# Gate and up of a gated MLP by Strassen's seven products for half of their K pairs, in an fp32 two-block kernel on one core

## The chip, the cores and the metric

One core of one Trainium2 chip runs the whole program as one launch. The metric is device time in microseconds (us). TensorE (PE) multiplies, VectorE (DVE), ScalarE (ACT) and GpSimd (POOL) do the elementwise work, SyncE (SP) issues the loads; POOL can issue loads as well.

## The reference

Two transformer blocks in fp32 on 256 tokens of width 2048 (16 meta tokens in front in the first block). What the change computes anew is the second block's gated MLP:

```python
def swiglu(h, w_gate, w_up, w_down):
    return (jax.nn.silu(h @ w_gate) * (h @ w_up)) @ w_down

def second_block(x, ...):
    h = h + hybrid_mixer(rms_norm(h, norm_mix[l]), ...)   # ends in: m @ w_out
    h = h + swiglu(rms_norm(h, norm_ffn[l]), w_gate[l], w_up[l], w_down[l])
    return rms_norm(h, norm_final)
```

w_gate and w_up are 2048 x 5632, w_down is 5632 x 2048, w_out is 2048 x 2048.

## The kernel before

Every fp32 product with weights is made of three products of parts: a number x is split into xh (12 significant bits) and xl (the rest), and x w is taken as xh wh + xh wl + xl wh. `load` fetches a piece of weights of 128 x 1024 (wr, 512 KB, issued by SP at L293), ACT copies it to the high part wh (L296), DVE subtracts to get the low part wl (L297). Raw pieces have 5 buffers, wh and wl 3 each, in one pool for the whole kernel.

Two shapes of product follow. `gemm_a` keeps weights stationary and streams 256 to 272 token columns (L304 to L306). `gemm_b` keeps 128 tokens stationary and streams 512 weight columns (L311 to L313) into one bank of PSUM for each of two token tiles. PSUM has four banks of tag g and four of tag a; a tag's banks go round in the order of first use in the program.

The second block ends like this. `branch` makes the three branches' outputs in four column blocks j; a branch's product is scaled on DVE (L979) and added to m on POOL (L980). For the last branch each j spawns `turn`, which transposes m on PE (L908) and splits it on ACT (L274) and DVE (L275) into mt. Then w2out (the mixing projection) runs over mt for four j, its result is added to the residual tiles htok (L1062), and another `turn` makes xn3, split and scaled, the input of the MLP.

`feed_forward_2` walks the 44 tiles of hidden width in two parts of 24 and 20. In a part, each block b (512 hidden columns, 11 in all) multiplies xn3 with gate (banks of tag g) and up (banks of tag a), 96 matmuls of 512 columns each; ACT applies silu straight from PSUM (L1087), DVE multiplies up's sums in (scalar_tensor_tensor, "stt", L1088) to get sl, and `turn` makes from it four split tiles at, with two banks of tag a and eight transposes. Then the part's down product over at follows for four column blocks, and DVE adds it to htok (L1104). The tail is a norm and the stores.

The program's order sets priorities; a scheduler orders each engine's instructions by it ahead of time, among those that are ready by its own costs. Work such as `turn` is spawned with a delay and placed between the steps of the large products. An engine runs its list in that order, so an instruction that waits holds all behind it.

The first block's end matters too. The last heads' attention runs while the first products of w1out (`gemm_a`, output blocks f) already stand between; `product(f)` in `mixing_1` is called ahead for f = 1 and 2, and the residual tiles ht are loaded by SP at L801.

## Time and profile before

| what | value |
|---|---|
| time, median of 3 runs | 2778.96 us (2778.73 to 2779.33) |
| span of the profiled execution | 2777.6 us |
| PE busy | 2760.7 us (99%) |
| DVE busy | 1573.4 us (57%) |
| ACT busy | 1292.5 us (47%) |
| POOL busy | 275.3 us (10%) |
| moved by DMA | 498.30 MB, mean 179 GB/s |

Busy time is the time in which an engine has work under way. PE's matmuls are pipelined: a matmul's own duration is longer than the distance to the next one's start, so the pace is read from starts in a timeline. The granted clock is 1.00 where the throttle gives TensorE its full 2.4 GHz. Durations of single instructions come from one profiled execution.

### The profile page before, as it was taken

What the parts mean: (1) busy time and instruction counts of PE and PEld (TensorE: products, weight loads), DVE (VectorE), ACT (ScalarE), POOL (GpSimd) and SP (SyncE); (2) the same over time, 40 slices, a digit from 0 to 9 for tenths busy, and PEclk for the clock granted to TensorE, in tenths of its full rate; (3) what the DMA queues carried; (4) which work ended last, traced back from release to release, by engine and by line L of the source; (5) the groups of instructions that cost most, each with busy time, mean ns of one, the idle gap of its engine ahead of it and who ended that gap; (6) DMA issues with size and microseconds to landing.
All of it is one profiled execution on the core that took longest, in us unless ns stands there. A gap on an engine that the chain in (4) does not pass through costs nothing.

```text
span 2777.6 us, 40930 instructions
## 1 busy us (share of the span) xinstructions
PE 2760.7 (99%) x16346; PEld 2425.5 (87%) x16346; DVE 1573.4 (57%) x2006; ACT 1292.5 (47%) x1768; POOL 275.3 (10%) x304
## 2 busy tenths in 40 slices
...
GB/s 234 161 125 120 109 195 182 183 182 184 188 189 183 184 185 185 182 181 178 182 189 185 192 188 170 168 180 184 182 182 189 182 189 183 188 189 184 190 195 151
DMA packets 142035, 498.30 MB, mean 179 GB/s; under 512 B 15890, under 2 KB 17427, under 8 KB 141843
## 3 DMA queue, kind: packets, MB, share of 16 engines
...
q8 instruction: 128, 2.10, 0.3%
q10 hardware_dynamic: 434, 0.78, 0.1%
...
## 4 chain that ended last, share of the span: by engine, by line
PE 99%; POOL 0%; DVE 0%; ACT 0%; DMA 0%; issue 0%; ACTq 0%; SPq 0%; POOLq 0%; DVEq 0%
PE ps L311 19%; PE ps L313 19%; PE ps L312 19%; PE ps L304 13%; PE ps L305 12%; PE ps L306 12%; PE ps L908 1%; PE ps L601 1%; PE ps L685 0%; PE ps L686 0%; PE ps L603 0%; PE ps L644 0%; POOL ht L811 0%; PE ps L574 0%; PE ps L1171 0%; DVE wl L297 0%
## 5 line engine op out<-in xcount | busy, mean ns | idle before, releaser
L297 DVE TENSOR_TENSOR wl<-wr,wh 128x1024 fp32r<-128x1024 f32 (+2 forms) x937 | 1148.7, 1227 | 1000.0 <-ACT wh L296 998.5
L296 ACT ACTIVATE wh<-wr 128x1024 fp32r<-128x1024 f32 (+2 forms) x937 | 979.8, 1046 | 1259.6 <-PE ps L313 788.2
L311 PE MATMUL ps<-wh,xn 128*128 128x512 f32 x1216 | 483.1, 397 | 0.0
L313 PE MATMUL ps<-wh,xn 128*128 128x512 f32 x1216 | 479.6, 394 | 0.0
L312 PE MATMUL ps<-wl,xn 128*128 128x512 f32 x1216 | 478.6, 394 | 0.0
L305 PE MATMUL ps<-xf,wh 128*128 128x258 f32 (+1 forms) x1408 | 398.2, 283 | 0.0
L304 PE MATMUL ps<-xf,wh 128*128 128x258 f32 (+1 forms) x1408 | 397.9, 283 | 0.0
L306 PE MATMUL ps<-xf,wl 128*128 128x258 f32 (+1 forms) x1408 | 396.1, 281 | 0.0
L311 PE MATMUL ps<-wh,at 128*128 128x512 f32 x704 | 278.9, 396 | 0.0
L313 PE MATMUL ps<-wh,at 128*128 128x512 f32 x704 | 277.6, 394 | 0.0
L312 PE MATMUL ps<-wl,at 128*128 128x512 f32 x704 | 277.4, 394 | 0.0
L313 PEld LDWEIGHTS ps<-wh,xn 128*128 128x128 f32 x1216 | 228.1, 188 | 54.4
L312 PEld LDWEIGHTS ps<-wl,xn 128*128 128x128 f32 x1216 | 228.5, 188 | 52.2
L311 PEld LDWEIGHTS ps<-wh,xn 128*128 128x128 f32 x1216 | 228.3, 188 | 51.6
L306 PEld LDWEIGHTS ps<-xf,wl 128*128 128x128 f32 x1408 | 267.8, 190 | 0.0
L305 PEld LDWEIGHTS ps<-xf,wh 128*128 128x128 f32 x1408 | 265.8, 189 | 0.1
L304 PEld LDWEIGHTS ps<-xf,wh 128*128 128x128 f32 x1408 | 265.0, 188 | 0.1
L304 PE MATMUL ps<-xn,wh 128*128 128x256 f32 x640 | 181.9, 284 | 0.0
L305 PE MATMUL ps<-xn,wh 128*128 128x256 f32 x640 | 179.7, 281 | 0.0
L306 PE MATMUL ps<-xn,wl 128*128 128x256 f32 x640 | 179.5, 280 | 0.0
L313 PEld LDWEIGHTS ps<-wh,at 128*128 128x128 f32 x704 | 132.2, 188 | 31.8
L311 PEld LDWEIGHTS ps<-wh,at 128*128 128x128 f32 x704 | 132.3, 188 | 30.7
...
## 6 DMA issues: line engine op xcount, KB each, us to landing
wr<-in_w1ff SPq DMA_DIRECT2D x176, 512.0 KB, 3.3
wr<-in_w2g SPq DMA_DIRECT2D x96, 512.0 KB, 3.4
wr<-in_w1down SPq DMA_DIRECT2D x88, 512.0 KB, 3.3
wr<-in_w2gate SPq DMA_DIRECT2D x88, 512.0 KB, 3.3
wr<-in_w2up SPq DMA_DIRECT2D x88, 512.0 KB, 3.3
wr<-in_w2down SPq DMA_DIRECT2D x88, 512.0 KB, 3.3
wr<-in_w2a SPq DMA_DIRECT2D x80, 512.0 KB, 3.3
wr<-in_w1in SPq DMA_DIRECT2D x48, 512.0 KB, 3.3
```

What stands on the lines that cost most here:

```text
L296: self.last_copy = nc.scalar.activation(h[:, d], raw[:, d], AF.Copy)
L297: nc.vector.tensor_tensor(l[:, d], raw[:, d], h[:, d].bitcast(F32), op=OP.subtract)
L304: mm(ps, wh, xh, start=first, stop=False)
L305: mm(ps, wh, xl, start=False, stop=False)
L306: mm(ps, wl, xh, start=False, stop=last)
L311: mm(ps, xh, wh, start=first, stop=False)
L312: mm(ps, xh, wl, start=False, stop=False)
L313: mm(ps, xl, wh, start=False, stop=last)
L601: PE.matmul(ps[:, :257], v01[:, b * 128:b * 128 + 128], ta[:, b * 257:b * 257 + 257], start=b == 0, stop=False)
L908: self.nc.tensor.transpose(ps[:, i * 256 + t * 128:i * 256 + t * 128 + 128], tiles[t][:, f * 128:f * 128 + 128], self.cs("ident"))
```

## The change

For four of the eight K pairs (two tiles of 128 rows each; `FAST` = pairs 0, 2, 4, 6) of gate and up, the 2 x 2 block product of (two token tiles) x (two K tiles) x (two halves of 256 columns) is made by Strassen's scheme with seven products instead of eight, in the form with shared sums. Each of the seven is again three products of parts, each with 128 x 128 stationary and 256 columns streaming (L1171). The other four pairs go on as before.

- The token side's sums are made once, in `turn_fast`: the transposed, scaled tile is copied to a raw tile, three subtractions follow, and four splits.
- The weight side's sums are made for each piece, in `load_fast`: SP loads y (128 x 512: two blocks' copies of b12) and x (128 x 768: b11, b21, b22), POOL issues a load of 128 x 512 that adds into y on arrival, and DVE makes two more sums of 256 columns (L1140, L1141). ACT and DVE then split 1024 columns of x and 768 of y (ACT L1143, DVE L1144).
- The result is put together at the end of a block in `gemm_fast`: own banks (tag g) take products that belong to one quarter alone, sums banks (tag a) the shared ones; two ACT copies (L1177) and seven DVE operations (L1180 to L1186) combine them. Silu and the stt read and write SBUF tiles then.
- Gate, then silu, then up, then the stt, each with two banks of either tag. The down product goes in four parts of 12, 12, 12 and 8 tiles.
- Pools: weights of attention_1 have their own; a pool `ph` holds the eight residual tiles; mixing_1 to mixer_2 use `wp2` and `p2`; w2out and the MLP use `wp3` (raw 6, wh and wl 5 each) and `p3`.

Comments and debug calls are left out of the diff, as are lines that only follow from them.

```diff
...
 FFN_PARTS = (24, 20)
-
-# columns of the packed vectors
+FFN_PARTS_2 = (12, 12, 12, 8)
...
+def pack_fast(w):
+
+
+
+    k, n = w.shape
+    b = w.reshape(k // 256, 2, 128, n // 512, 2, 256).transpose(3, 0, 1, 4, 2, 5)
+    f = b[:, list(FAST)]
+    b11, b12, b21, b22 = (f[:, :, i, j] for i in range(2) for j in range(2))
+    rest = [p for p in range(k // 256) if p not in FAST]
+    r = w.reshape(k // 256, 2, 128, n // 512, 512).transpose(3, 0, 2, 1, 4)[:, rest]
+    cat = lambda *x: np.concatenate(x, axis=-1)
+    return cat(b11, b21, b22), cat(b12, b12), cat(b11, b22), r.reshape(r.shape[:3] + (1024,))
+
...
-    f["w2gate"] = pack_b(i["w_gate_2"][0])
-    f["w2up"] = pack_b(i["w_up_2"][0])
+    for k, v in (("w2gate", "w_gate_2"), ("w2up", "w_up_2")):
+        for x, p in zip("xyap", pack_fast(i[v][0])):
+            f[k + x] = p
...
     def mid(self, name, w=512, dtype=F32):
-        tag, bufs = ("m1", 10) if w <= LP else ("m15", 8) if w <= 384 else ("m2", 17)
-        return self.p2.tile([128, w], dtype, name=name, tag=tag, bufs=bufs)
+        i = 0 if w <= LP else 1 if w <= 384 else 2 if w <= 2 * LP else 3
+        return self.p2.tile([128, w], dtype, name=name, tag="m%d" % i, bufs=self.n_mid[i])
...
             self.cst = cp.tile([128, NCST], F32, name="cst")
             self.mb = cp.tile([1, NH * NM], F32, name="mb")
-            with tc.tile_pool(name="p1", bufs=1) as self.p1:
+            with tc.tile_pool(name="wp", bufs=1) as self.wp, tc.tile_pool(name="p1", bufs=1) as self.p1:
                 self.attention_1()
-            with tc.tile_pool(name="p2", bufs=1, reuse_waits="tile") as self.p2:
-                self.mixing_1()
-                self.feed_forward_1()
-                if "stop1" in a:
-                    return
-                self.mixer_2()
-                self.feed_forward_2()
-
-    # ---- block 1 ----
+            with tc.tile_pool(name="ph", bufs=1, reuse_waits="tile") as self.ph:
+                with tc.tile_pool(name="wp2", bufs=1, reuse_waits="tile") as self.wp, \
+                        tc.tile_pool(name="p2", bufs=1, reuse_waits="tile") as self.p2:
+                    self.mixing_1()
+                    self.feed_forward_1()
+                    mt = self.mixer_2()
+                self.n_w = (6, 5)
+                self.n_mid = (0, 0, 6, 2)
+                with tc.tile_pool(name="wp3", bufs=1, reuse_waits="tile") as self.wp, \
+                        tc.tile_pool(name="p3", bufs=1, reuse_waits="tile") as self.p2:
+                    self.mixing_2(mt)
+                    self.feed_forward_2()
+
...
-        self.xn = xn3 = []
+        return mt
+
+    def mixing_2(self, mt):
+        a, htok, V = self.a, self.htok, self.nc.vector
+        self.xn, self.forms = xn3, forms = [], {}
         for j in range(4):
             pss = [self.bank(), self.bank()]
...
-            for h in (0, 1, 2, 7):
-                self.dbg(n + str(h), [y[h]])
+            self.spawn(self.turn_fast(j, xn3, forms, self.gains("norm_ffn", j)), 2.0)
+
+    def turn_fast(self, j, out, forms, g):
+
+
+        S, V = self.nc.scalar, self.nc.vector
+        for c in range(2):
+            ps = self.bank(tag="a")
+            for i in range(2):
+                for t in range(2):
+                    f = 2 * c + i
+                    self.nc.tensor.transpose(ps[:, i * 256 + t * 128:i * 256 + t * 128 + 128],
+                                             self.htok[t][j][:, f * 128:f * 128 + 128], self.cs("ident"))
+            if 2 * j + c not in FAST:
+                for i in range(2):
+                    hl = self.pair(T, "xn3")
+                    self.split_scaled(hl[:, 0, :T], hl[:, 1, :T], ps[:, i * 256:i * 256 + 256], g(2 * c + i))
+                    out.append(hl)
+                yield 0.5
+                continue
+            raw = self.mid("raw", 1024).rearrange("p (f t) -> p f t", f=8)
+            for i in range(2):
+                S.activation(raw[:, 2 * i:2 * i + 2], ps[:, i * 256:i * 256 + 256].rearrange("p (f t) -> p f t", f=2), AF.Copy,
+                             scale=g(2 * c + i))
+            yield 1.0
+            V.tensor_tensor(raw[:, 4:6], raw[:, 1:2].to_broadcast([128, 2, 128]), raw[:, 0:4:3], op=OP.subtract)
+            V.tensor_tensor(raw[:, 6], raw[:, 0], raw[:, 5], op=OP.subtract)
+            V.tensor_tensor(raw[:, 7], raw[:, 2], raw[:, 6], op=OP.subtract)
+            yield 1.0
+            parts = []
+            for i in range(4):
+                hl = self.pair(T, "xn3")
+                self.split(hl, raw[:, 2 * i:2 * i + 2].rearrange("p f t -> p (f t)"), T)
+                parts.append(hl)
+                yield 0.5
+            forms[2 * j + c] = [(p[:, 0, x], p[:, 1, x]) for p in parts for x in (slice(0, 128), slice(128, 256))]
+            out += parts[:2]
+            yield 0.5
+
+    def load_fast(self, a, b, i):
+
+
+        nc = self.nc
+        x, y = (self.wp.tile([128, 1024], F32, name="wr", tag="wr", bufs=self.n_w[0]) for _ in range(2))
+        hx, hy = (self.wp.tile([128, 1024], F32R, name="wh", tag="wh", bufs=self.n_w[1]) for _ in range(2))
+        lx, ly = (self.wp.tile([128, 1024], F32R, name="wl", tag="wl", bufs=self.n_w[1]) for _ in range(2))
+        nc.sync.dma_start(y[:, :512], self.a[a + "y"][b, i])
+        nc.sync.dma_start(x[:, :768], self.a[a + "x"][b, i])
+        nc.gpsimd.dma_start(y[:, :512], self.a[a + "a"][b, i], accum_op=OP.add)
+        nc.vector.tensor_tensor(x[:, 768:], y[:, :256], x[:, 512:768], op=OP.add)
+        nc.vector.tensor_tensor(y[:, 512:768], x[:, 768:], x[:, 256:512], op=OP.add)
+        for r, h, l, n in ((x, hx, lx, 1024), (y, hy, ly, 768)):
+            nc.scalar.activation(h[:, :n], r[:, :n], AF.Copy)
+            nc.vector.tensor_tensor(l[:, :n], r[:, :n], h[:, :n].bitcast(F32), op=OP.subtract)
+        return (hx, lx), (hy, ly)
+
+    def gemm_fast(self, a, b, xt):
+
+
+        S, V = self.nc.scalar, self.nc.vector
+        mm = self.nc.tensor.matmul
+        own, sums = [self.bank() for _ in range(2)], [self.bank(tag="a") for _ in range(2)]
+        lo, hi = slice(0, 256), slice(256, 512)
+        rest = [p for p in range(KT // 2) if p not in FAST]
+        for i, (p, f) in enumerate(zip(rest, FAST)):
+            h, l = self.load(self.a[a + "p"][b, i])[0]
+            for j in range(2):
+                for t in range(2):
+                    xh, xl = xt(2 * p + j, t)
+                    self.cam(own[t], xh, xl, h[:, j * 512:j * 512 + 512], l[:, j * 512:j * 512 + 512], i == 0 and j == 0,
+                             p == rest[-1] and j == 1)
+                self.tick(1.3)
+            wx, wy = self.load_fast(a, b, i)
+            A11, A21, A12, A22, S7, S1, R, S4 = self.have_form(f)
+            for n, (ps, c, x, w, o) in enumerate((
+                    (sums[0], lo, A11, wx, 0), (own[0], lo, A12, wx, 256), (own[0], hi, S4, wx, 512),
+                    (sums[1], lo, S1, wy, 0), (sums[1], hi, S7, wy, 256), (sums[0], hi, R, wx, 768),
+                    (own[1], lo, A22, wy, 512))):
+                o = slice(o, o + 256)
+                for u, v in ((0, 0), (0, 1), (1, 0)):
+                    mm(ps[:, c], x[u], w[v][:, o], start=i == 0 and u == v and n in (0, 3),
+                       stop=f == FAST[-1] and u == 1, skip_group_check=True)
+                self.tick(0.36)
+
+        e = self.mid("e", 1024)
+        for k in range(2):
+            S.activation(e.rearrange("p (a b) -> p a b", a=4)[:, k:k + 3:2], sums[k].rearrange("p (a b) -> p a b", a=2), AF.Copy)
+        q1, q5, q6, q7 = (e[:, k * 256:k * 256 + 256] for k in range(4))
+        o = [self.mid("sl") for _ in range(2)]
+        V.tensor_tensor(q6, q6, q1, op=OP.subtract)
+        V.tensor_tensor(q7, q7, q6, op=OP.add)
+        V.tensor_tensor(o[1][:, lo], own[1][:, lo], q7, op=OP.subtract)
+        V.tensor_tensor(q7, q7, q5, op=OP.add)
+        V.tensor_tensor(q5, q5, q6, op=OP.add)
+        V.tensor_tensor(o[0], own[0], e[:, :512], op=OP.add)
+        V.tensor_tensor(o[1][:, hi], own[1][:, hi], q7, op=OP.add)
+        return o
+
+    def have_form(self, f):
+        while f not in self.forms:
+            self.force()
+        return self.forms[f]
 
...
-        for part in FFN_PARTS:
+        for part in FFN_PARTS_2:
             at = []
             for b in range(f0 // 4, (f0 + part) // 4):
-                pg, pu = [self.bank() for _ in range(2)], [self.bank(tag="a") for _ in range(2)]
-                for ps, n in ((pg, "w2gate"), (pu, "w2up")):
-                    for q in range(4):
-                        self.gemm_b(ps, self.load(a[n][b, q]), range(4 * q, 4 * q + 4), xt, q == 0, q == 3)
-                sl = [self.mid("sl") for _ in range(2)]
+                sl = self.gemm_fast("w2gate", b, xt)
                 for t in range(2):
-                    last_silu = S.activation(sl[t], pg[t], AF.Silu, scale=r[:, t:t + 1])
+                    last_silu = S.activation(sl[t], sl[t], AF.Silu, scale=r[:, t:t + 1])
+                pu = self.gemm_fast("w2up", b, xt)
+                for t in range(2):
                     V.scalar_tensor_tensor(sl[t], pu[t], r[:, t:t + 1], sl[t], op0=OP.mult, op1=OP.mult)
                 self.spawn(self.turn(sl, at, "at2"), 2.0)
             last = f0 + part == FT
...
```

How the order moves instructions at three places (names carry tile numbers; ps are PSUM banks, cst the identity for transposes):

On PE, the last product of mixer 2 (yc) and the start of w2out (mt). Before:

```order
L311 MATMUL ps_19907<-wh_19916,mt_19211 128x512
L312 MATMUL ps_19907<-wl_19917,mt_19211 128x512
L313 MATMUL ps_19907<-wh_19916,mt_19211 128x512
L311 MATMUL ps_19908<-wh_19916,mt_19211 128x512
L312 MATMUL ps_19908<-wl_19917,mt_19211 128x512
L313 MATMUL ps_19908<-wh_19916,mt_19211 128x512
L908 MATMUL ps_19939<-cst_68,m_15760 128x128
L908 MATMUL ps_19939<-cst_68,m_15762 128x128
L908 MATMUL ps_19939<-cst_68,m_15760 128x128
L908 MATMUL ps_19939<-cst_68,m_15762 128x128
L311 MATMUL ps_19907<-wh_19916,mt_19214 128x512
L312 MATMUL ps_19907<-wl_19917,mt_19214 128x512
```

After:

```order
L329 MATMUL ps_19837<-wh_19881,yc_19031 128x512
L330 MATMUL ps_19837<-wl_19882,yc_19031 128x512
L331 MATMUL ps_19837<-wh_19881,yc_19031 128x512
L932 MATMUL ps_19954<-cst_65,m_15767 128x128
L932 MATMUL ps_19971<-cst_65,m_15767 128x128
L932 MATMUL ps_19954<-cst_65,m_15769 128x128
L932 MATMUL ps_19954<-cst_65,m_15767 128x128
L932 MATMUL ps_19954<-cst_65,m_15769 128x128
L932 MATMUL ps_19971<-cst_65,m_15769 128x128
L932 MATMUL ps_19971<-cst_65,m_15767 128x128
L932 MATMUL ps_19971<-cst_65,m_15769 128x128
L329 MATMUL ps_19922<-wh_19925,mt_19201 128x512
```

The transposes of m stood between products of w2out; now all eight stand ahead of the first of them, whose high part comes on ACT behind the mt splits:

```order
L314 ACTIVATE wh_19875<-wr_19874 128x1024
L314 ACTIVATE wh_19881<-wr_19880 128x1024
L292 ACTIVATE mt_19959<-ps_19954 128x256
L292 ACTIVATE mt_19962<-ps_19954 128x256
L292 ACTIVATE mt_19976<-ps_19971 128x256
L292 ACTIVATE mt_19979<-ps_19971 128x256
L314 ACTIVATE wh_19925<-wr_19924 128x1024
L314 ACTIVATE wh_19931<-wr_19930 128x1024
```

wh_19881 belongs to the last yc product and wh_19925 to the first of w2out.

On SP, the loads of w1out at the end of attention. Before:

```order
L293 DMA wr_4097<-in_w1out 128x1024
L293 DMA wr_4103<-in_w1out 128x1024
L293 DMA wr_4370<-in_w1out 128x1024
L293 DMA wr_4376<-in_w1out 128x1024
L293 DMA wr_4452<-in_w1out 128x1024
L293 DMA wr_4458<-in_w1out 128x1024
L293 DMA wr_4541<-in_w1out 128x1024
L293 DMA wr_4547<-in_w1out 128x1024
L293 DMA wr_4623<-in_w1out 128x1024
L801 DMA ht_4368<-in_ht 128x548
```

After:

```order
L311 DMA wr_4097<-in_w1out 128x1024
L311 DMA wr_4103<-in_w1out 128x1024
L825 DMA ht_4375<-in_ht 128x548
L311 DMA wr_4377<-in_w1out 128x1024
L311 DMA wr_4383<-in_w1out 128x1024
L311 DMA wr_4459<-in_w1out 128x1024
L311 DMA wr_4465<-in_w1out 128x1024
L825 DMA ht_4537<-in_ht 128x548
L311 DMA wr_4548<-in_w1out 128x1024
L311 DMA wr_4554<-in_w1out 128x1024
```

The load of the residual tile ht stood behind nine w1out loads; it now stands behind two.

On PE, the end of the first gate and up (sl are the tiles that `turn` transposes). Before, 12 matmuls behind up's last:

```order
L311 MATMUL ps_21258<-wh_21262,xn3_20111 128x512
L312 MATMUL ps_21258<-wl_21263,xn3_20111 128x512
L313 MATMUL ps_21258<-wh_21262,xn3_20111 128x512
L908 MATMUL ps_21285<-cst_68,sl_21251 128x128
L908 MATMUL ps_21285<-cst_68,sl_21252 128x128
L908 MATMUL ps_21285<-cst_68,sl_21251 128x128
L908 MATMUL ps_21285<-cst_68,sl_21252 128x128
L311 MATMUL ps_21257<-wh_21268,xn3_20125 128x512
L312 MATMUL ps_21257<-wl_21269,xn3_20125 128x512
L313 MATMUL ps_21257<-wh_21268,xn3_20125 128x512
```

After, 39 matmuls behind up's last:

```order
L1171 MATMUL ps_21170<-wh_21270,xn3_20362 128x256
L1171 MATMUL ps_21170<-wl_21272,xn3_20362 128x256
L1171 MATMUL ps_21170<-wh_21270,xn3_20362 128x256
L932 MATMUL ps_21192<-cst_65,sl_20925 128x128
L932 MATMUL ps_21192<-cst_65,sl_20926 128x128
L932 MATMUL ps_21192<-cst_65,sl_20925 128x128
L932 MATMUL ps_21192<-cst_65,sl_20926 128x128
L1171 MATMUL ps_21172<-wh_21205,xn3_20141 128x256
L1171 MATMUL ps_21172<-wl_21207,xn3_20141 128x256
L1171 MATMUL ps_21172<-wh_21205,xn3_20141 128x256
L932 MATMUL ps_21224<-cst_65,sl_20925 128x128
```

The transposes of sl moved from behind 12 matmuls of the next gate to behind 39 of it, and the next gate's first products into sums banks (ps_21172) stand behind them.

## Rows read from the trace of the kernel before

**Rows 1.** The page's head, and its engines' busy time.
```profile
span 2777.6 us, 40930 instructions
...
PE 2760.7 (99%) x16346; PEld 2425.5 (87%) x16346; DVE 1573.4 (57%) x2006; ACT 1292.5 (47%) x1768; POOL 275.3 (10%) x304
```

**Rows 2.** Windows, gate and up of one part: busy time of each engine, granted clock, DMA share, GB/s.
```profile
2030.00:2180.00 150.00, 150.00 (x660) 121.41 (x659) 74.31 (x75) 65.72 (x74) 0.00 (x0) 1.00 0.56 187
```

**Rows 3.** Timeline, PE, second MLP: start, us; 43 matmuls of 512 columns apart.
```profile
2029.81 0.40 PE L311 MATMUL ps<-wh,xn 128*128 128x512 f32 x1
...
2039.80 0.39 PE L312 MATMUL ps<-wl,xn 128*128 128x512 f32 x1
```

**Rows 4.** Timeline, PE, block 2's input projection: 35 matmuls of 256 columns apart.
```profile
1239.78 0.28 PE L304 MATMUL ps<-xn,wh 128*128 128x256 f32 x1
...
1243.89 0.28 PE L306 MATMUL ps<-xn,wl 128*128 128x256 f32 x1
```

**Rows 5.** Groups by line and form, DVE, then ACT: busy us, mean ns of one, idle before.
```profile
L297 DVE TENSOR_TENSOR wl<-wr,wh 128x1024 fp32r<-128x1024 f32 x896 | 1106.3, 1235 | 990.0 <-ACT wh L296 988.7
...
L275 DVE TENSOR_TENSOR at<-gu,at 128x256 fp32r<-128x256 f32 x44 | 18.4, 419 | 0.5 <-ACT at L274 0.5
...
L1088 DVE SCALAR_TENSOR_TENSOR sl<-ps,rn,sl 128x512 f32<-128x512 f32 x22 | 15.4, 744 | 0.0
...
L1104 DVE TENSOR_TENSOR htok<-htok,ps 128x512 f32<-128x512 f32 x16 | 10.3, 681 | 3.3 <-PE ps L313 3.3
...
L296 ACT ACTIVATE wh<-wr 128x1024 fp32r<-128x1024 f32 x896 | 949.2, 1060 | 1235.8 <-PE ps L313 785.1 <-issue 221.5 <-PE ps L305 217.8
...
L782 ACT ACTIVATE htok<-ps 128x512 f32<-128x512 f32 x8 | 4.7, 592 | 2.1 <-PE ps L780 2.1
```

**Rows 6.** Timeline, end of attention: SP's w1out issues, then PE at f=1's products.
```profile
298.57 0.33 SPq L293 DMA_DIRECT2D wr<-in_w1out  x1
...
323.14 0.38 PE L578 MATMUL ps<-cst,p 128*128 128x128 f32 x2
...
323.61 0.37 PE L304 MATMUL ps<-mix,wh 128*128 128x258 f32 x1
...
328.81 0.28 PE L304 MATMUL ps<-mix,wh 128*128 128x258 f32 x1
```

**Rows 7.** Timeline, end of mixer 2: DVE, POOL, PE, ACT.
```profile
1928.98 1.28 DVE L979 TENSOR_TENSOR sg<-ps,sg 128x512 f32<-128x512 f32 x2
...
1929.74 3.54 POOL L980 TENSOR_TENSOR m<-m,sg 128x512 f32<-128x512 f32 x2 [30.79 <-DVE sg L979]
...
1933.54 0.60 PE L908 MATMUL ps<-cst,m 128*128 128x128 f32 x4
...
1934.18 0.38 ACT L274 ACTIVATE mt<-ps 128x256 fp32r<-128x256 f32 x1 [0.78 <-PE ps L908]
```

**Rows 8.** Timeline, PE at the kernel's start: matmuls of 258 columns.
```profile
6.74 0.42 PE L305 MATMUL ps<-xg,wh 128*128 128x258 f32 x1
...
7.82 0.42 PE L305 MATMUL ps<-xg,wh 128*128 128x258 f32 x1
...
11.35 0.28 PE L306 MATMUL ps<-xg,wl 128*128 128x258 f32 x1
```

**Rows 9.** Windows around the last matmul: PE busy, granted clock, DMA share, GB/s.
```profile
2772.00:2773.00 1.00, 0.00 (x0) 0.85 1.02 391
2773.00:2775.00 2.00, 0.00 (x0) 0.50 0.94 349
```

**Rows 10.** DMA issues: queue, count, KB each, median us from issue to landing.
```profile
wr<-in_w1out SPq DMA_DIRECT2D x32, 512.0 KB, 3.4
...
wr<-in_w1lat SPq DMA_DIRECT2D x15, 448.0 KB, 5.2
...
wr<-in_wkvup SPq DMA_DIRECT2D x8, 256.0 KB, 3.6
...
wr<-in_w2p SPq DMA_DIRECT2D x4, 256.0 KB, 2.7
```

17 lines of the change are left out of this document (8 added, 9 removed).

## The prediction

> **What bounds the kernel now.** First the page's head: PE is busy 2760.7 of 2777.6 us [rows 1]; the 17 us left are the first load and the tail. Then the windows inside the second MLP: PE full, DVE 74.3 of 150 us, ACT 65.7, POOL nothing, the DMA engines 56% at 187 GB/s [rows 2]. So PE's own instructions are the time, and everything else has slack. The reader should see two things: less PE work is worth its full time only while DVE, the loads and the order keep weight pieces ready, and DVE has about half of its time left there, no more.
>
> **PE's gain.** A matmul of 512 columns starts every 9.99 / 43 = 0.232 us [rows 3], one of 256 columns, with a new stationary tile each time, every 4.11 / 35 = 0.1174 us [rows 4]. A fast pair of K tiles (256 rows by 512 columns, two token tiles) had 12 matmuls of 512 columns, 2.79 us, and has 21 of 256, 2.47 us: 0.32 us less. There are 4 pairs x 2 weights x 11 blocks b = 88 of them: **-28.5 us**. The other pairs, the down product and its count of matmuls (four parts for two) stay. PE's work per b falls from 45.5 us (192 x 0.2326 and 0.9 for eight transposes, four of them 0.60 with their overlap [rows 7]) to about 42.95.
>
> **What DVE gets.** Per plain pair plus fast pair it makes the low parts of 1024, 1024 and 768 columns and two sums of 256: 1.235 + 1.235 + 0.96 + 2 x 0.42 = 4.27 us (0.96 lies on the line through 256 and 1024 columns [rows 5]). PE takes 2.79 + 2.47 = 5.26 for the same pairs. Every gate or up block ends in seven more operations, six of 256 columns and one of 512 from PSUM, 6 x 0.42 + 0.68 = 3.2 us, and a b has two stt (0.74) and four at splits (0.42). A b is 8 x 4.27 + 2 x 3.2 + 1.49 + 1.67 = 43.7 us of DVE, where before it was 16 x 1.235 + 1.49 + 1.67 = 22.9. DVE becomes as long as PE there. The down products, at half DVE load [rows 2], let it lead by a few pieces (five wh and wl), so this alone costs little. ACT has 16 high parts of 1.06 and 8 of some 0.83, four copies, two silus and four splits, 29 us a b.
>
> **The stall between up and the next gate.** Before, gate and up wrote different banks, and a transposed tile came from an stt straight after up. Now the turn of b holds the tag-a banks ahead of the next gate's sums, and the order puts on PE, behind up: 12 matmuls of 512, 9 of 256, 12 of 512, 6 of 256 (7.35 us), then the transposes of sl. Sl is ready after ACT's two copies (0.59 each) and, in DVE's order, seven combines, two stt, and two low parts of 1024 that stand among them: 1.18 + 3.2 + 1.49 + 2 x 1.235 = 8.3 us [rows 5]. PE waits 0.9 us per b: 11 x 0.9 = **+9.9 us**. Bounds: +4, if combines start early, and +20, if DVE comes 0.9 us late to up's end (two sums stand ahead of the combines in its queue).
>
> **The way into the mixing projection of block 1.** The new tiles for the residual stream lie on released places, and SP's queue now has a residual load behind the first two w1out loads, waiting for the last head's softmax and transposes at 323.2 us; all other w1out loads stand behind it. Before they were issued from 298.6 on, and PE filled 323.6 to 328.8 with their products while the last head finished [rows 6]. Now issue, load [rows 10] and high part [rows 5] make 323.2 + 0.4 + 3.4 + 1.06 = 328.1, and with the second wait of SP's queue some 329 to 330; about **+4 us** go idle (2 to 6).
>
> **The way into w2out.** Its weight tiles are a new pool on mixer_2's places, and ACT has the four mt splits ahead of w2out's first high part, so nothing of w2out runs until the last mt exists. In the trace the last two m products leave DVE from 1928.98, POOL adds them from 1929.74 for 3.54 us, the transposes start at 1933.54, and the mt splits follow on ACT from 1934.18 [rows 7], 0.38 there and 0.42 on DVE [rows 5], one behind the other; PE meanwhile ran w2out. Now PE is empty from 1929.1: 4.2 us to POOL's end, 0.9 of transposes, 2.65 of splits (four halves on ACT of 0.38, two or three on DVE between them), 1.06 for the high part, about 8.8 us, in two stretches. At the start of the kernel PE came out of an idle stretch with matmuls of 258 columns every 1.08 / 5 = 0.216 us, double the 0.117 [rows 4], and their durations fell to 0.28 only at 11.35 us [rows 8]: of 5.9 us about 2.8 lost; some us after the kernel's last matmul the granted clock is 0.85 in 2772 to 2773 and then 0.50, its lower level of 1.2 GHz [rows 9]. One such loss goes on top: **+11.6 us**; bounds 5 (idle filled by the scheduler's other work, clock kept) and 14.5.
>
> **Small terms.** Three subtractions and four low parts per transformed tile in w2out fall on DVE's slack, except those for the last column block, ahead of the first gate: **+1 us** (0 to 2). The down parts' extra adds (0.68 us each [rows 5]) run beside matmuls; the tail is unchanged.
>
> **The accumulating load, unseen before.** Each fast pair brings y (256 KB) by SP, then a second 256 KB by POOL that adds into y, and both DVE sums wait for it. Bounds for each from rows: 2.7 us (a 256 KB load of block 2) to 3.6 for the first, 2.7 to 5.2 (448 KB into a busy start) for the second [rows 10], so 5.4 to 8.8 for the trip; I take 2.7 + 3.6 = 6.3, the row of the same block and the dearest 256 KB row. The raw slots allow two iterations: y of iteration i+2 goes out when x of i is split, and DVE has 0.96 + 4.27 + 1.235 = 6.47 us of work before it needs the sum. At 6.3 it costs **0**. Past 6.47, six of the eight trips of a b show and each is shared by two iterations: 3 us per b and us of trip, less some 14 us in all that the leads cover (four parts, each entered with two of the five pieces ready beyond the one in use and those being made, 2 x 1.75 us of PE). A trip of 7.0 costs 3 x 0.53 x 11 - 14 = 3, 7.5 costs 3 x 1.03 x 11 - 14 = 20, 8.5 costs 53, and the far end of 8.8 costs 63.
>
> The Trainium skill, DMA: Bandwidth & Descriptors, section Anatomy of one DMA, has 2.0 us plus bytes / 436e3 for a load issued by GpSimd: an estimate of 2.6 us for this one, without the add. By it the trip would be 5.3 and the term 0 as well; no run of before shows it.
>
> In bytes: 1408 KB per two pairs for 1024 at 187 GB/s in 5.6 us is about 272 GB/s, 82% of the engines by the 56% row. Should adding cost a second pass of its 256 KB, it is 96%, a third, full.
>
> **Sum.** -28.5 + 9.9 + 4 + 11.6 + 1 + 0 = -2.0 us. The profiled execution has a span of 2777.6 and the median is 2778.96; the 1.4 us around the span stay. **2777 us.** A measurement can tell 0.2%, 5.6 us: faster is under 2773.4, slower over 2784.5.
>
> **Rivals.**
> *The stalls are smaller (faster).* Place: w2out's start and the up to gate seam. If POOL's adds and the mt splits keep the first high part only 5 us late and combines get ahead (4 us), the sum is -28.5 + 4 + 2 + 5 + 1 = -16.5: 2762. It decides from the point where idle per b is under 0.5 us. For it: the windows show DVE's slack is there in the down parts. Against: the order is fixed and DVE's queue has no free place at up's end.
> *The accumulating trip sets the loop (slower).* Place: L1140 at the head of DVE's queue, with splits and combines of the same PE block behind it. It decides from a trip of 7.0 us; at 7.5 to 8.5 the time is 2797 to 2830. For it: an accumulating transfer reads its target as well, and 448 KB took 5.2 us [rows 10]. Against: 512 KB took 3.4 elsewhere in the same rows.
> The Trainium skill, SBUF — State Buffer, the trap "DVE blocks DMA", says that GpSimd cannot write the descriptors of a load it issues while a DVE instruction in a two-port mode holds the port they share; the same page has a tensor_tensor of two SBUF inputs contend with GpSimd's reads alone. By the first half the trip would be longer by up to one DVE instruction, 7.5 us with 1.2 us on 6.3 [rows 5]; no run of before issues such a load, and the second half speaks against it here, since DVE's long instructions are tensor_tensors.
> *The DMA engines fill.* If the adding pass costs three times its bytes, 1920 KB per iteration at 333 GB/s take 5.9 us, over PE's 5.26: 88 iterations x 0.64 = 56 us less what the down parts refill and what the loop had free, 2785 to 2815. At two passes the load is 96% and costs a few us.
>
> **Chances.** The forecast, 2767 to 2787, 0.45 (of it 0.13 faster, 0.22 same, 0.10 slower). Smaller stalls, 2757 to 2767, 0.17. The trip sets the loop, 2785 to 2835, 0.27, of it 0.02 within 0.2%. Full DMA engines, 0.11: 0.02 faster, 0.09 slower. Faster 0.32, same 0.24, slower 0.44. The range 2762 to 2815 leaves out about half of the fastest case and the longest trips. Sides are near even, so the forecast's own range stands beside it: 2767 to 2787.
>
> **What would show it.** PE's fast matmuls 0.117 us apart (else the gain is wrong). Idle PE before the turn's transposes of about 0.9 us, eleven times, waiting for DVE's stt. In the w2out start one idle of 4 us for POOL's m and one of 4 for a high part, then matmuls at half pace. PE waiting near 323 to 330 for w1out. L1140 waiting little for the accumulating DMA, with a median landing of 3.6 us or less; if it is over 4 and DVE idles for it in gate and up, the second rival has it. DMA share in gate and up about 0.8; if 0.95 and over, the third. DVE at 95% or more in gate and up.

## The result, and the profile after

The changed kernel takes 2926.43 us (median of 4 runs, 2920.08 to 2928.05), the kernel before beside it 2778.85 (2778.72 to 2779.33): ratio 1.0527, 95% interval 1.0514 to 1.0540. It is slower by 147.6 us; the forecast was 2777 and the range ended at 2815. The profiled execution of after is its fastest (2920.08), so the traces below differ by less, 140.7 us of span.

The page's head of after, its queues and its chain of the work that ended last (the answers to [rows 1]):

```profile
span 2918.3 us, 43844 instructions
...
PE 2785.9 (95%) x17138; PEld 2473.9 (85%) x17138; DVE 1782.3 (61%) x2460; ACT 1384.7 (47%) x1921; POOL 350.9 (12%) x392
...
q0 software_dynamic: 12672, 23.07, 5.1%
...
DMA 14%; PE 11%; DVE 6%; issue 2%; ACT 1%; POOLq 0%; ACTq 0%; DVEq 0%
```

PE was busy for 99% and is busy for 95%: 132 us of the span are without a matmul, where there were 17. PE's own busy time rose too, by 25 us, although matmul work was taken from it. The chain of the last work ran through PE for 99% of the span; after's chain can be followed back over the last third of the span only, from w2out on, and there it runs through the DMAs first.

Where the time went is read from the first and last start of single lines that close a stage. Of before, then of after: the first add of MLP 1, w2out's adds, the down product's adds of MLP 2 (duration min/median/max, first and last start).

```profile
L853 DVE TENSOR_TENSOR gg<-ps,rf x44: 418/427/428, 435.9 to 1054.5; 128x258 f32<-128x258 f32 x44
...
L1062 DVE TENSOR_TENSOR htok<-htok,ps x8: 678/680/680, 1952.2 to 2022.2; 128x512 f32<-128x512 f32 x8
...
L1104 DVE TENSOR_TENSOR htok<-htok,ps x16: 678/681/686, 2328.7 to 2768.6; 128x512 f32<-128x512 f32 x16
```

```profile
L877 DVE TENSOR_TENSOR gg<-ps,rf x44: 417/427/428, 445.9 to 1064.5; 128x258 f32<-128x258 f32 x44
...
L1090 DVE TENSOR_TENSOR htok<-htok,ps x8: 680/680/682, 1970.1 to 2040.2; 128x512 f32<-128x512 f32 x8
...
L1227 DVE TENSOR_TENSOR htok<-htok,ps x32: 680/681/689, 2221.9 to 2904.8; 128x512 f32<-128x512 f32 x32
```

The way into block 1's mixing cost 445.9 - 435.9 = 10.0 us. The way into w2out cost 1970.1 - 1952.2 - 10.0 = 7.9. From w2out's last add to the last down add there were 746.4 us and now there are 864.6: +118.2 in the second MLP. The tail went from 2777.6 - 2768.6 = 9.0 us to 13.5: +4.5. Together 140.6.

What PE and DVE waited for in after (total us, times, longest), and one window of its second MLP (start:end, length, then busy us of PE, PEld, DVE, ACT and POOL, granted clock, DMA share, GB/s):

```profile
PE ps L330 <- DVE wl L315: 60.4, 27, 6.3
PE ps L1171 <- DVE wl L1144: 33.1, 18, 4.8
```

```profile
DVE wr L1140 <- DMA wr<-in_w2gatea: 95.7, 34, 6.0
DVE wr L1140 <- DMA wr<-in_w2upa: 79.1, 34, 5.8
```

```profile
2300.00:2400.00 100.00, 82.42 (x454) 71.03 (x453) 69.10 (x104) 43.42 (x54) 12.08 (x14) 0.90 0.74 201
```

PE waits for low parts, and DVE, which makes them, waits for the adding load at L1140. PE is empty for 17.6 us of these 100, DVE for 31, and the clock granted is 0.90; [rows 2] had PE full at 1.00. The DMA engines are at 0.74 and not full.

The chain of waits in after shows one lap of the loop in the up block from 2128 us on (start, duration; pieces on DVE, ACT or in a DMA):

```profile
2128.52 1.13 DVE wl L1144
...
2129.68 4.35 DMA wr<-in_w2upy
...
2134.65 5.62 DMA wr<-in_w2upa
2140.29 0.44 DVE wr L1140
...
2140.89 1.07 ACT wh L1143
2141.98 1.24 DVE wl L1144
```

The low part of x frees its raw slot, SP loads a y into it, POOL then issues the adding load, DVE sums, ACT and DVE split, and that low part frees the next slot. The trip, from y's issue to the adding load's landing, is 10.59 us of it: 4.35 for y, 0.62 until POOL's issue starts, 5.62 for the adding load. The lap takes 2141.98 - 2128.52 = 13.46 us. Six raw slots at three a pair hold two pairs, so a pair comes every 6.73 us, and PE needs 5.26. Eight pairs a b at 1.47 us make 11.8 us above PE's time; the b's around here, taken from stt to stt (2101.67, 2159.09, 2210.47), took 57.4 and 51.4, against the 43.15 of the kernel without the adding load (e1, the first experiment).

### The profile page after: what moved, and what is told of

The parts are those of the page before. It is cut to its first block, busy times and chain, and to the rows that moved or that the text cites. A ratio compares the mean times of both kernels' runs of the same rounds, so it can differ in the third digit from the quotient of the medians.

```text
span 2918.3 us, 43844 instructions
## 1 busy us (share of the span) xinstructions
PE 2785.9 (95%) x17138; PEld 2473.9 (85%) x17138; DVE 1782.3 (61%) x2460; ACT 1384.7 (47%) x1921; POOL 350.9 (12%) x392
## 3 DMA queue, kind: packets, MB, share of 16 engines
q0 software_dynamic: 12672, 23.07, 5.1%
## 5 line engine op out<-in xcount | busy, mean ns | idle before, releaser
L315 DVE TENSOR_TENSOR wl<-wr,wh 128x1024 fp32r<-128x1024 f32 (+2 forms) x849 | 1037.9, 1225 | 707.8 <-ACT wh L314 706.1
L314 ACT ACTIVATE wh<-wr 128x1024 fp32r<-128x1024 f32 (+2 forms) x849 | 884.7, 1044 | 1032.2 <-PE ps L331 547.0
L330 PE MATMUL ps<-wl,xn 128*128 128x512 f32 x864 | 353.4, 409 | 60.4 <-DVE wl L315 60.4
L329 PE MATMUL ps<-wh,xn 128*128 128x512 f32 x864 | 350.8, 406 | 0.0
L331 PE MATMUL ps<-wh,xn 128*128 128x512 f32 x864 | 348.8, 404 | 0.0
L1143 ACT ACTIVATE wh<-wr 128x1024 fp32r<-128x1024 f32 (+1 forms) x176 | 161.0, 947 | 234.8 <-DVE wr L1140 176.4
L330 PEld LDWEIGHTS ps<-wl,xn 128*128 128x128 f32 x864 | 168.1, 195 | 104.7 <-DVE wl L315 69.4
L1171 PE MATMUL ps<-wh,xn 128*128 128x256 f32 x1232 | 245.5, 289 | 2.0 <-ACT wh L1143 1.9
L1171 PE MATMUL ps<-wl,xn 128*128 128x256 f32 x616 | 179.7, 292 | 33.3 <-DVE wl L1144 33.1
L1171 PEld LDWEIGHTS ps<-wh,xn 128*128 128x128 f32 x1232 | 203.1, 195 | 9.2 <-ACT wh L1143 5.3
L331 PEld LDWEIGHTS ps<-wh,xn 128*128 128x128 f32 x864 | 167.9, 194 | 38.9
L1144 DVE TENSOR_TENSOR wl<-wr,wh 128x1024 fp32r<-128x1024 f32 (+1 forms) x176 | 187.2, 1086 | 19.9 <-ACT wh L1143 19.9
L329 PEld LDWEIGHTS ps<-wh,xn 128*128 128x128 f32 x864 | 167.7, 194 | 35.3
```

Source lines behind the costliest of these rows:

```text
L314: self.last_copy = nc.scalar.activation(h[:, d], raw[:, d], AF.Copy)
L315: nc.vector.tensor_tensor(l[:, d], raw[:, d], h[:, d].bitcast(F32), op=OP.subtract)
L329: mm(ps, xh, wh, start=first, stop=False)
L330: mm(ps, xh, wl, start=False, stop=False)
L331: mm(ps, xl, wh, start=False, stop=last)
L1143: nc.scalar.activation(h[:, :n], r[:, :n], AF.Copy)
```

## Experiments

**What the adding load costs, and in what part of it (e1, e2, e3).** Three kernels: the first leaves the adding load out, so that y lacks its second term; the second loads the same bytes by POOL without adding, so that y holds only the second term; the third has after's pools, with MLP 2's products as before.

```diff
-        nc.gpsimd.dma_start(y[:, :512], self.a[a + "a"][b, i], accum_op=OP.add)
...
-        nc.gpsimd.dma_start(y[:, :512], self.a[a + "a"][b, i], accum_op=OP.add)
+        nc.gpsimd.dma_start(y[:, :512], self.a[a + "a"][b, i])
...
-FAST = (0, 2, 4, 6)
+FAST = ()
...
-                sl = self.gemm_fast("w2gate", b, xt)
+                        self.gemm_b(ps, self.load(a[n][b, q]), range(4 * q, 4 * q + 4), xt, q == 0, q == 3)
```

> As the changed kernel, but the POOL-issued load that adds into y is left out, so y lacks its second term in all 88 fast pairs; every other instruction stays. Theory A (the trip y, then the adding load, sets the loop: 3.8 + 0.9 + 4.8 us at the median in the trace of after against 6.5 us of cover) expects the trip to fall to y's 3.8 us and the second MLP to come to what the sum without it gave: about 2778.9 + 10 (way into mixing of block 1) + 8 (way into w2out) - 28.5 + 9.9 + 1 = 2779 us, 2770 to 2795. Rival B (DVE's load and its fixed order, with the turn between up and gate, cost the time) expects less than 30 us off 2926, above 2895.

> As the changed kernel, but POOL's load writes into y instead of adding to it, so y holds only its second term; bytes from memory, order and waits stay. If the adding itself is slow (theory A1) the landing falls from 4.8 us to about 3.5 and the time to 2830 to 2870. If it is the second load in a chain, whatever it does (theory A2), landing stays over 4.3 us and the time over 2895.

> The pools and the split of mixer 2 as in the changed kernel, but gate and up with the plain products and FFN parts of 12, 12, 12 and 8. The traces of before and after differ by 10.0 us at the first product of the first MLP and by 17.9 at w2out's first add, so 2778.9 + 18 = 2797 us, 2793 to 2801, if the pools alone cause these. If the scheduler's order changes with Strassen's part, 2779 to 2785.

Measured: 2775.51, 2840.50 and 2797.0 us, the kernel before beside them 2779.09. Here and below, a time without an interval is of a single run; after's four runs lie within 8 us. Without the load the kernel is as good as forecast, and the load costs 2926.4 - 2775.5 = 151 us. A plain load in its place costs 65 of them, and the adding itself the other 86. Not all of it is the trip: the scheduler orders e1 anew, and e1's tail takes 9.0 us where after's and e2's take 13.5 (why stands below). In the second MLP alone, measured as above, e1 has 723.9 us, e2 784.5 and after 864.6, so 61 for the load and 80 for the adding. The pools cost 17.9; read at the same lines, 8.4 on the way into block 1's mixing and 9.3 on the way into w2out, after's 10.0 and 7.9 in sum. The DMA issues of after, then of e2 (KB each, median us to landing), and e2's queue of such loads:

```profile
wr<-in_w2gatey SPq DMA_DIRECT2D x44, 256.0 KB, 3.4
wr<-in_w2gatea POOLq DMA_DIRECT2D x44, 256.0 KB, 4.7
wr<-in_w2upy SPq DMA_DIRECT2D x44, 256.0 KB, 4.3
wr<-in_w2upa POOLq DMA_DIRECT2D x44, 256.0 KB, 5.3
```

```profile
wr<-in_w2gatey SPq DMA_DIRECT2D x44, 256.0 KB, 3.0
wr<-in_w2gatea POOLq DMA_DIRECT2D x44, 256.0 KB, 3.4
wr<-in_w2upy SPq DMA_DIRECT2D x44, 256.0 KB, 3.6
wr<-in_w2upa POOLq DMA_DIRECT2D x44, 256.0 KB, 4.0
```

```profile
q0 software_dynamic: 7040, 23.07, 2.6%
```

The two landings add up to 8.1 us for gate and 9.6 for up, with e2's at 6.4 and 7.6, and some 0.6 us lie between them. Taken for each of the 88 pairs from y's issue to the second load's landing, the trip of after is 7.1 to 12.5 us, median 9.6, and e2's has a median of 7.7. An adding load takes the DMA engines twice as long for its bytes as a plain one (5.1% for 2.6%) in 1.8 times the packets.

e1 also answers for the rest of the sum: a b takes 43.15 us (stt at 2134.55 and 2177.70). Its page's head, and its window of 100 us in gate and up:

```profile
PE 2740.8 (99%) x17138; PEld 2448.3 (88%) x17138; DVE 1781.0 (64%) x2460; ACT 1383.8 (50%) x1916; POOL 273.4 (10%) x304
```

```profile
2060.00:2160.00 100.00, 98.27 (x621) 87.88 (x620) 90.57 (x138) 63.45 (x79) 0.00 (x0) 1.00 0.70 216
```

DVE is busy for 90.57 of 100 us, and PE for 98.27. With the same 17138 matmuls PE is busy 2740.8 us here at a mean granted clock of 0.996, and 2785.9 in after at 0.981: 45 us of the load's price are matmuls made slower by the clock, and most of the rest is PE without work.

**The old pools kept (e4, e5).** Raw pieces stay in the pool of the whole kernel (5 raw, 3 high, 3 low), and y gets a pool of its own (3 raw, 2, 2). The second kernel leaves out the adding load besides, with y short of its second term again.

```diff
+NY = (3, 2)
...
+        y = self.p2.tile([128, 768], F32, name="yr", tag="yr", bufs=NY[0])
+        hy = self.p2.tile([128, 768], F32R, name="yh", tag="yh", bufs=NY[1])
+        ly = self.p2.tile([128, 768], F32R, name="yl", tag="yl", bufs=NY[1])
```

> Strassen's part as changed, but the weight pool is kept open for the whole kernel as before (5 raw, 3 high, 3 low) and the y pieces have a pool of their own (3 raw of 768 columns, 2 high, 2 low), so that nothing of w2out waits for mixer 2's places and y goes out up to three iterations ahead. If the loop's cost is the trip against its cover (theory A), 10 + 8 us go and most of the loop's 147 us too: 2765 to 2800. If DVE's load and order set it (theory B), only the 18 us go: 2900 to 2910.

> As e4_pools_kept without the POOL-issued adding load, so y lacks its second term in all 88 fast pairs. If the losses add up, it is e1's 2775.5 less the 17.9 us that the pools cost: 2757.6 us, 2754 to 2763. If e1 owed something to its six raw buffers, 2765 to 2785.

Measured: 2838.47 and 2777.12. e4 lies between its two ranges and fits neither; e5 lies in its second, that e1 owed something to its six raw buffers. The 17.9 us are back, but x and the plain pieces share five raw slots and three high and low ones: in e4 DVE waits for x (29.7 and 24.0 us) beside the adding load (41.3 and 27.3), and in e5 b's take 46 and 43 us in turn. That the fewer slots are the cause is argued; the order of DVE, counted below, is a rival for e4.

**The add on an engine.** On e4's pools SP brings both halves of y in one load of 512 KB, and POOL (e6, three y slots) or DVE (e8, two) adds them.

```diff
-        nc.gpsimd.dma_start(y[:, :512], self.a[a + "a"][b, i], accum_op=OP.add)
+        nc.gpsimd.tensor_tensor(y[:, :512], y[:, :512], y[:, 512:], op=OP.add)
```

> As e4_pools_kept, but y and its second term come in one plain load of 512 KB by SP and POOL adds the halves (128 x 512, 1.3 to 2.3 us in the trace of before). Theory A (it was the trip): load 4.4 and add about 2, 6.4 us instead of 10, with three raw slots it is covered: 2757 to 2765, below both kernels. Rival (POOL's adds and DVE's stand in each other's way, DVE being 90% busy in e1's gate and up): DVE falls behind, 2775 to 2800.

> As e6_add_on_pool (two raw slots for y instead of three), the add made by DVE. DVE then has 43.7 + 8 x 0.69 = 49.2 us per b against 43.15 of PE. If DVE's busy time sets the loop when it is longer: 2757.6 + 11 x 6.0 less up to 14 us of lead from the down parts, 2808 to 2824. If the order hides part of it, 2775 to 2808.

Measured: 2817.36 (ratio 1.0141, 1.0125 to 1.0158) and 2807.17. e6 is above both of its ranges, and e8 at the border of its two. Groups by line and form of DVE in e5, then in e6 (busy us, mean ns of one, idle before):

```profile
L1145 DVE TENSOR_TENSOR wl<-wr,wh 128x1024 fp32r<-128x1024 f32 x88 | 107.3, 1219 | 16.8 <-ACT wh L1144 16.7
L1145 DVE TENSOR_TENSOR yl<-yr,yh 128x768 fp32r<-128x768 f32 x88 | 83.6, 950 | 0.1
```

```profile
L1146 DVE TENSOR_TENSOR wl<-wr,wh 128x1024 fp32r<-128x1024 f32 x88 | 117.2, 1332 | 4.9 <-ACT wh L1145 4.8
L1146 DVE TENSOR_TENSOR yl<-yr,yh 128x768 fp32r<-128x768 f32 x88 | 108.2, 1229 | 0.1
```

Beside POOL's adds the same DVE instructions take 1332 for 1219 ns and 1229 for 950; in e8, which has the same load and no adds on POOL, they take 1220 and 950, so it is POOL's adds that lengthen them. Eighty-eight adds lengthen DVE by 9.9 and 24.6 us there alone, so the engine that had slack took it from the one that had none.

**Fewer fast pairs (e7, e9 to e11).** On e4's pools. With two fast pairs of eight (pairs 1 and 5, three plain pairs between them) a trip has more work to hide behind. e9 adds a change of the tail: the table for the last norm is loaded behind both of the last silus, and not between them. e10 has three fast pairs, with two, two and one plain pairs ahead of them, e11 the same with the add on DVE; both have e9's tail.

```diff
-FAST = (0, 2, 4, 6)
+FAST = (1, 5)
...
-                self.pin_exp_ln(last_silu)
+                pin = S.preload_act_table_set("natural_log_exp_and_others")
+                for s in silus:
+                    self.after(pin, s)
...
-FAST = (1, 5)
+FAST = (1, 3, 5)
```

> As e4_pools_kept with the adding load, but two fast pairs of eight (1 and 5) instead of four: three plain pieces stand ahead of each fast pair. PE's gain is half of the 25.4 us that e1's 43.15 us per b show, 12.7. Theory A: the loop of two trips in flight, (10 + 3) / 2 = 6.5 us, is under the 10.8 us that PE takes for three plain pairs and a fast one: 2766, 2763 to 2772. Rival C (each adding load costs its own price wherever it stands, e4 less e5 over 88 of them, 0.9 us): 2806, 2795 to 2815.

> As e7_two_pairs_kept, with the load of the exp and ln table held behind both last silus instead of one. In e7's tail ACT loads tables four times, 1.28 us each, and the last store ends 4.5 us later behind the last product than before. If that is all of the tail, 2774.1 - 4.5 = 2769.6 us, 2768 to 2771. If the loads only move elsewhere, 2774.

> As e9 with three fast pairs (1, 3, 5), two, two and one plain pieces ahead of them. PE's gain is three quarters of 25.4, 19.0 us. Theory A: two trips in flight take (10 + 3) / 2 = 6.5 us a pair, PE gives 7.1 (5/3 x 2.79 + 2.47): just covered, 2760, 2758 to 2766. Rival D (the kept pools with 3 high and 3 low pieces are too short, as e5's 2777.1 instead of 2757.6 suggests): 2768 to 2790.

> As e10, but y and its second term in one load and the add on DVE, as e8. No load issued by POOL is left. DVE has 2 x (5 x 1.235 + 3 x 3.73) + 9.6 = 44.3 us a b, PE 43.7. Theory A (DVE's time or PE's, whichever is longer): 2779.1 - 19 + 7 less the lead from the down parts, 2758 to 2770. Rival D (short pools and order): 2775 to 2800.

Measured: e7 2774.10. e9 2768.68 (5 runs, 2768.51 to 2770.16) beside 2778.99 for before: ratio 0.9965, 0.9952 to 0.9977, so it is faster than both kernels, by 10 us or 0.35% than before. e10 2816.11 (1.0126, 1.0110 to 1.0141), e11 2794.94 (1.0061, 1.0047 to 1.0074). Among e7's waits of DVE for DMAs the adding load does not appear (x does, with 30.7 and 25.5 us), and a b takes 44.35 us: the gain is half of e1's 2.3 us, for half the pairs. e7 ended 2 us above its range and e9 in its own; e10 was above both of its ranges, and e11 in its rival's. At three pairs DVE waits for x (55.6 and 50.1 us in e10, 25.3 and 27.7 in e11). Whether the slots or DVE's order make it wait is not separated by a run; the count below speaks for the order as well.

**More slots, and the order (e12 to e18).** e12 has nine raw slots and three high and low, e16 nine and five (the first lines of the diff). e17 is e16 with the first sum of each fast pair (L1140) held behind the low parts of the pair before in DVE's order; nothing else is changed. e13 to e15 give x and y three raw slots each on the kept pools, for four, three and two fast pairs, with all high and low parts in three slots; e18 is e13 with y's own high and low slots, and with the order held as in e17.

```diff
-                self.n_w = (6, 5)
-                self.n_mid = (0, 0, 6, 2)
+                self.n_w = (9, 5)
+                self.n_mid = (0, 0, 6, 1)
...
-        nc.vector.tensor_tensor(x[:, 768:], y[:, :256], x[:, 512:768], op=OP.add)
+        s1 = nc.vector.tensor_tensor(x[:, 768:], y[:, :256], x[:, 512:768], op=OP.add)
+        for o in getattr(self, "last_low", ()):
+            self.after(s1, o)
+        self.last_low = []
...
-            nc.vector.tensor_tensor(l[:, :n], r[:, :n], h[:, :n].bitcast(F32), op=OP.subtract)
+            self.last_low.append(nc.vector.tensor_tensor(l[:, :n], r[:, :n], h[:, :n].bitcast(F32), op=OP.subtract))
```

> The changed kernel with 9 raw buffers instead of 6 and 3 high and 3 low instead of 5 and 5 in the last weight pool, nothing else: three fast pairs of loads in flight instead of two. Theory A (a pair comes every trip plus 3 us over the trips in flight): (10 + 3) / 3 = 4.3 us, under PE's 5.26, so most of the 151 us that e1 lacks go: 2775 to 2820. Rival C (the adding loads themselves can't come faster): 2890 to 2930.

> Four fast pairs, the weight pool kept open, x and y with three raw buffers of their own each, plain pieces with five, high and low shared with three each, the table held behind both silus. Theory A with the raw slots as the cause: neither the trip nor x's load is late, PE sets 43.2 us a b: 2779 - 25.4 + 3 = 2757, up to 2775 where three high and low pieces are short. If the trip isn't hidden by three slots: 2810 to 2840 as e4.

> As e13 with three fast pairs (1, 3, 5). Theory A: 2779 - 19 + 2 = 2762, 2758 to 2772. If e10's 2816 came from something else than x's raw slots: over 2800.

> As e9_two_pairs_tail with e13's buffers. Nothing waited for loads in e9's gate and up on PE, so no change: 2768.7, 2767 to 2771.

> The changed kernel with 9 raw buffers instead of 6 (and one e tile of 1024 instead of two, for room); high and low stay at five each, which e12 had cut to three. Slots as the only cause (theory A): 2775 to 2820. Order as the cause (theory E: with more slots the fixed order on DVE puts the sum of pair i+1 or i+2 ahead of the low parts of pair i, so that a late adding load holds the low parts whose end releases the next slots): no better than 2926, 2890 to 2960.

> As e16, but each pair's first sum is held behind the low parts of the pair before in DVE's order; nothing else. Theory E: three pairs are in flight for a trip of about 10 us, (10 + 3) / 3 = 4.3 us under PE's 5.26, and the second MLP is PE bound as in e1: 2775 to 2800. If order doesn't matter: the same as e16.

> Four fast pairs, the weight pool kept open (5 raw, 3 high, 3 low), x and y with three raw buffers each of their own, y with two high and two low of its own, the sums held behind the low parts of the pair before, the table behind both silus. Theory E: 2757.5 and the few us by which 3 high and low are short, 2755 to 2772, below e9's 2768.7 or near it. If the order isn't the cause: 2830 to 2985 as e4 and e13.

Measured: e12 2978.39, e13 2984.78 (1.0736, 1.0720 to 1.0752), e14 2917.19 (1.0494, 1.0479 to 1.0510), e15 2806.69 (1.0098, 1.0081 to 1.0115), e16 2930.39, e17 2789.49, e18 2794.64 (1.0055, 1.0038 to 1.0071). e12 to e15 missed: with more raw slots the trip was to be hidden, and all four are above their ranges, by 36 to 210 us. e16 and e17 came out as theory E has it, and e18 23 us above its range. A half more raw slots gave nothing (e16 against 2926.4), where slots alone as the cause had to give most of the 151 us. DVE's order in e16 shows why. Of two pairs, wr_21448 and wr_21502 are the x pieces; wl_21452 is the first pair's low part:

```order
L1140 TENSOR_TENSOR wr_21448<-wr_21449,wr_21448 128x256
L1140 TENSOR_TENSOR wr_21502<-wr_21503,wr_21502 128x256
L1141 TENSOR_TENSOR wr_21449<-wr_21448 128x256
L315 TENSOR_TENSOR wl_21432<-wr_21430,wh_21431 128x1024
L1144 TENSOR_TENSOR wl_21452<-wr_21448,wh_21450 128x1024
```

The timeline of these on DVE in e16, the fourth left out (start, duration, idle before and what ended it):

```profile
2116.70 0.41 DVE L1140 TENSOR_TENSOR wr<-wr 128x256 f32<-128x256 f32 x1
2123.65 0.42 DVE L1140 TENSOR_TENSOR wr<-wr 128x256 f32<-128x256 f32 x1 [6.54 <-DMA wr<-in_w2upa]
2123.99 0.42 DVE L1141 TENSOR_TENSOR wr<-wr 128x256 f32<-128x256 f32 x1
...
2125.46 1.22 DVE L1144 TENSOR_TENSOR wl<-wr,wh 128x1024 fp32r<-128x1024 f32 x1
```

The first pair is on the chip at 2116.70, but its second sum and its low part stand behind the second pair's first sum, and so behind a load that lands 6.5 us later. The scheduler used the new slots to get further ahead, so they hid no more of the trip. Counted on DVE over each whole trace, a pair's first sum starts before the low parts of all older pairs have started at 27 of 88 pairs in after and in e2, at 77 in e16, 84 in e12, 87 in e13, and at none in e17 and e18; at 70 in e4; with two pairs at 1 of 44 in e9 and 43 of 44 in e15, with three at 62 of 66 in e10. In e17 (there L1144 is the second sum and L1147 the low part):

```profile
2105.24 2.09 DVE L1147 TENSOR_TENSOR wl<-wr,wh 128x1024 fp32r<-128x1024 f32 x2 [0.72 <-ACT wh L1146]
...
2108.39 0.42 DVE L1140 TENSOR_TENSOR wr<-wr 128x256 f32<-128x256 f32 x1
...
2110.07 2.10 DVE L1147 TENSOR_TENSOR wl<-wr,wh 128x1024 fp32r<-128x1024 f32 x2 [0.81 <-ACT wh L1146]
```

There each pair's sums and low parts are through before the next pair's sum. DVE's waits for the adding load of e16, then of e17, and that load's landing in e17:

```profile
DVE wr L1140 <- DMA wr<-in_w2gatea: 137.1, 36, 7.5
DVE wr L1140 <- DMA wr<-in_w2upa: 93.8, 22, 6.7
```

```profile
DVE wr L1140 <- DMA wr<-in_w2gatea: 18.7, 10, 2.8
```

```profile
wr<-in_w2gatea POOLq DMA_DIRECT2D x44, 256.0 KB, 5.8
wr<-in_w2upa POOLq DMA_DIRECT2D x44, 256.0 KB, 5.9
```

141 us by the order alone, while the load in e17 lands in 5.8 and 5.9 us, no sooner than in e16 (5.0 and 5.8). The trip was not shortened; it was hidden. e17's second MLP takes 734.2 us, 12 less than before's 746.4; that e17 is still slower as a whole lies in the two ways in (17.9) and the tail (4.5). The waits in e12 (115.8 and 89.1 us on the same load) and e13 (96.5 and 110.5) read like e16's. e15 has e9's fast pairs and e9's tail, with more raw slots, and is 38 us slower: 29 in the second MLP, where its order runs ahead and e9's does not, and 9 on the way into w2out. That three high and low slots cost e12 its other 48 us beside e16, and e18 what it lacks against its expectation, was only argued. Not run: the held order with after's six raw slots, so how much of the 151 us the order alone makes there stays open (78.6 of after's 174.8 us of waits for the adding load stand at its 27 pairs that run ahead), and e17's order with the old pools' 17.9 us saved and enough high and low slots.

## Why the prediction was wrong, point by point

**The accumulating load: the step that failed.** The sum had a trip of 6.3 us against 6.47 of cover, and 0 for the term. The trip was 9.6 us at the median: y lands in 3.4 to 4.3 and not 2.7, some 0.6 us pass until POOL's issue, which the sum did not have, and the adding load takes 4.7 to 5.3 and not 3.6. The upper bound of 8.8 was under it as well: 2.7 and 3.6 came from rows where the DMA engines have less to do (a share of 0.54 where the 2.7 was read, 0.74 in after's gate and up), and the 5.2 row was taken for an outer end. That the traffic makes the landings longer is argued. The prediction's own formula gives 3 x 3.16 x 11 - 14 = 90 us for a trip of 9.63, and PE waited 98 us in the second MLP; for e2's 7.74 it gives 28, and PE waited 46 there. So its mechanism and slope were about right for the waits, and the size of the trip was not. The second rival had the place (L1140 at the head of DVE's queue), and its time ended nearly 100 us too early. What neither held: that DVE's list has L1140 of one pair ahead of the low parts of the one before. In after that is so at 27 of 88 pairs, and at 77 with nine raw slots (e16). And idle PE costs more than its length: beside the 98 us of waits, 45 went in matmuls at a lower granted clock, for which the formula had no term; together they are the 118 + 25 that the MLP lost against its own gain.

The 2.6 us by the Trainium skill, DMA: Bandwidth & Descriptors, section Anatomy of one DMA, was for a load without an add; such a load took 3.4 to 4.0 in e2 and its adding form 4.7 to 5.3, so the measurement decides against the figure here.

**PE's gain and the stall behind up: right together, the stall mis-sized.** -28.5 and +9.9 made -18.6; e1 has 45.46 - 43.15 = 2.31 us a b, 25.4 in all. Fast matmuls start 0.117 us apart, as in [rows 4]. The stall is about 0.15 us a b, not 0.9 (PE waits 1.7 us in all for sl in e1): the second stt ends 7.24 us after up's last matmul, where the sum of DVE's durations had 8.3. The durations listed overlap: 256-column operations are listed with 0.42 and start 0.34 apart when one follows the other. The second MLP of e1 as a whole gains 22.5 us, 2.9 less than its b's.

**DVE as long as PE: about right.** DVE has 90.57 of 100 us in e1, where 95 or more was told, and it costs PE little.

**The way into block 1's mixing: 10.0 for 4 (2 to 6).** The order of SP was read rightly, and ACT's was not read. PE, ACT and SP of after at that place:

```profile
337.00 0.58 PE L322 MATMUL ps<-mix,wh 128*128 128x258 f32 x1 [7.14 <-ACT wh L314]
```

```profile
335.49 0.51 ACT L296 ACTIVATE xf<-ht,cols 128x258 fp32r<-128x258 f32 x1 [3.32 <-POOL ht L835]
335.91 1.99 ACT L314 ACTIVATE wh<-wr 128x1024 fp32r<-128x1024 f32 x2
```

```profile
323.72 4.89 SPq L311 DMA_DIRECT2D wr<-in_w1out  x4
```

SP issues w1out at 323.72 as forecast, and its pieces land from 330.13 on; but the second high part stands on ACT behind a split of ht. That split waits for POOL's add into ht (L835), and the add waits for DVE's scaled product (wo, L834, done at 333.84), not for the load of ht, which had landed at 326.18. So the rest of the delay is ACT's order. PE then came out of 7.1 us of idle at half pace: matmuls of 258 columns start 0.215 us apart (granted clock 0.50 from 330 to 338, 0.73 from 338 to 346). e3 has the same wait of 7.1 us, so the pools make it.

**The way into w2out: 7.9 for 12.6 with its small term, inside the bounds.** PE waits there for POOL's m and then 3.17 us for the high part, as told; POOL's two adds took 2.48 us, not 3.54 [rows 7].

**"The tail is unchanged": wrong, 4.5 us.** ACT in after's tail has four loads of a function table, each of 1.28 us. Between the last two silus, and then one of the four:

```profile
2838.94 1.28 ACT L384 ACT_TABLE_LOAD   x1
2840.23 1.28 ACT L1208 ACT_TABLE_LOAD   x1
...
2905.01 1.28 ACT L362 ACT_TABLE_LOAD   x1
```

Before's tail has none. In after's order the table for the norm is loaded between the last two silus (L384); the silu behind it loads its own again (L1208), and the tail pays. It stood in ACT's order and was not read there. e9's tail, with the table behind both silus, has none, and e9 is 5.4 us faster than e7. e1 and e16 have the table behind both silus by the scheduler's choice, and tails of 9.0 and 9.2 us; e2 and e17 have it between them, and 13.5.

**What came out without the load:** read at the same lines, e1 has +10.5 and +8.0 on the two ways in, -22.5 in the second MLP and 0 in the tail, together -4.0, and -3.6 in its time. The forecast for this part was -2.0, of +4, +12.6, -18.6 and 0. That the two sums agree is luck: the terms were off by 4 to 7 us, one upward and two downward.

**The third rival, full DMA engines: no.** After has 0.74, and e17, which hides the trip, 0.89 at 256 GB/s (2050 to 2200 us). The adding load does cost its second pass. **Descriptors held up by DVE:** POOL's issue took 0.86 us each time in the stretch from 2105 to 2148 us, with DVE's tensor_tensors around it. The Trainium skill, SBUF — State Buffer, has, in the trap "DVE blocks DMA", a wait for two-port modes, of which no run here shows any. The Trainium skill, SBUF — State Buffer, section Who interferes with whom, has a tensor_tensor with both inputs in SBUF contend with GpSimd's reads, and e6's 1229 ns for e8's 950 agree.
